# Hybrid decoder step on one core: a third key buffer, earlier gathers, closer decode steps and a re-spaced sample chain in the MLP

## Chip, cores and metric

One core of a Trainium2 chip runs the whole kernel. The metric is the device time of one execution in microseconds (us). Engines: PE is TensorE (PEld its weight loads), DVE is VectorE, ACT is ScalarE, POOL is GpSimd, SP is SyncE, which here only issues DMAs.

## What is computed

One layer of a decoder for two inputs at once: a prompt of 512 new tokens, and a sample of 8 sequences with one new token each, of which every one attends to 4096 cached tokens. Cut to what matters here:

```python
h = rmsnorm(x, g_pre_mix); q, k, v, logf, ..., gates = split(h @ w_in)
o_fox = forgetting_attention(q, k, v, logf)      # prompt: 512 x 512 causal
                                                 # sample: cache_k/cache_v[page_table], 4096 rows, 8 heads x 64
o_gla = gated_linear_attention(...)
u  = sigmoid(gfox) * (o_fox @ w_fox_out) + sigmoid(ggla) * (o_gla @ w_gla_out)
x  = x + rmsnorm(u @ w_o, g_post_mix)            # d_model 1024
h2 = rmsnorm(x, g_pre_mlp)
y  = x + rmsnorm(square(relu(h2 @ w_up)) @ w_down, g_post_mlp)   # d_ff 4096
```

Everything is float32. The paged cache that the sample reads is 8 x 32 pages of 128 rows, 64 MB of keys and 64 MB of values.

## The kernel before

**Dense work.** Every weight matrix is taken in units of 256 columns. A unit is loaded by SP (tile raw, four loads of 256 KB, up to two units ahead), split into a rounded high part (wh, ACT, L222) and the rest (wl, DVE, L223), and multiplied three times by PE (high x high, high x low, low x high) into PSUM tiles pmm. The MLP has four chunks c of 1024 hidden columns; each has an up half (four units, function up) and a down half (four units, function down). The prompt's 512 tokens are columns 0 to 511 of the transposed activations, and the 8 sample tokens can ride along as columns 512 to 519 where they are known in time.

**Decode.** The sample's attention to its cache is a Python generator, decode (from L549), of 144 steps: b counts 0 to 8, g 0 to 15. In a step with b < 8 the key page group of sequence b is gathered by POOL with an indirect DMA (tile kk, 512 KB, two buffers, L209), multiplied by the query (DVE, L574) and summed over the head dimension (DVE, L575). In a step with b > 0 the values of sequence b-1 are used: every second step one gathered value tile (tile kv, 1 MB, two buffers) goes through PE against the exponentials pt (tile pdv). So steps 1 to 128 have keys, and the last 16 have values alone. At the end of a sequence a chain over DVE, PE and ACT makes the exponentials (L604 to L621).

**How the steps are laid out among the dense work.** Each matmul adds its columns over 2400 to a planner's clock (L82). After each piece of dense work (a yield, in the MLP mostly 24 matmuls of 512 columns, so 5.12 us of that clock) pump(rate) pays clock x rate / TAU into an account and emits one decode step for each 1 in it; TAU is 3.1. The rates are PA to PD and PF before the MLP, PG = 1.5 in the first four yields of the MLP, and PE_ = 1 after them. LK and LV say how many steps ahead of its use a key or value gather is emitted (0 and 2). This is the order of emission. The framework then orders each engine's instructions by priority of emission, and lets a later one pass an earlier one whose inputs or buffer are not there yet in its own timeline; on the chip each engine runs that fixed order.

**The sample's path through the end.** When decode has ended, start_mix puts the generator sample_mix on the list side; beside(1) advances it once per yield of dense work. It projects the attention output with w_fox_out (four pieces) and w_o (four pieces), one per advance, with weights loaded again by SP into kv tiles (sload); then sample_post and sample_sum do the first norm and the residual sum, rsqrt (DVE and POOL, L217 and L218) the scale, and norm_T_sample (L333) scales x on DVE and transposes it in eight small PE transposes (L339) into h2S and, by split, into columns 512 to 519 of h2 and l2. From then on mixed[0] is true. Up units taken before that have no sample columns; they and the down units of the same chunk are put on the list late, and sample_mlp does them for the sample alone, one per advance, with the unit's weights loaded a second time into kv tiles (two loads of 512 KB each). The list whole marks a chunk of which any up unit was late; all four of its down units are then late too. sample_end, at the last down unit, drains the rest.

**Names of the rows.** px<-kv,c is a late unit's product on PE, px<-sel,td the sum over its four column groups, pd<-ident,qb the sample's transposes, pdv<-kv,pt decode's values, pmm<-h,wh and pmm<-wh,c and their like the dense units.

Of the kernel before, what the change touches and what calls it, by code (L numbers as in the profile page):

```python
# [17 lines left out]
D = 1024  # L18
T = 512
NB = 8  # L20
# [4 lines left out]
TS = T + NB  # L25
TR = 544
FP, LP, LQ = 3, 1, 1
PA, PB, PC, PD, PE_ = 1, 1.2, 0.6, 0.6, 1
LK, LV = 0, 2
TO = 1  # L30
PF, PG, HN = 0.8, 1.5, 2
BU = dict(h=4, c8=9, wh=6, wl=5, raw=5, kk=2, kv=2, td=2, ts=5, qb=2, tj=1, ev=1)
PK = 2
TAU = 3.1
MS = 1
# [15 lines left out]
def _emit(ctx, tc, I, O):  # L51
# [494 lines left out]
    oS = cst([128, 4, 32], "oS")  # L546
    G.memset(oS, 0.0)

    def decode():  # L549
        steps = [(b, g) for b in range(NB + 1) for g in range(NG)]  # L550
        pk, pv_ = [], []
# [1 line left out]
        lf = logf_load(0)  # L553
        bias = None
        for i, (b, g) in enumerate(steps):
            while nk <= min(i + LK, NB * NG - 1):
                pk.append(page_load(kvw, ixki, nk // NG, nk % NG, KJ, "kk"))
                nk += 1
            while nv <= NB * NV - 1 and NG + nv * VJ // KJ <= i + LV:
# [83 lines left out]
    def pump(rate):  # L643

        owed[0] += (clock[0] - seen[0]) * rate / TAU
        while owed[0] >= 1 and (scored[0] or count[0] < NG):
            owed[0] -= 1
            count[0] += 1
            if next(dec, "end") == "end":
                over[0] = True  # L650
        seen[0] = clock[0]
# [570 lines left out]
    def sample_mix():  # L1222
        x, y = new_["x"], new_["y"] = [[new([8, 512], "ts") for _ in range(2)] for _ in range(2)]
        V.tensor_scalar(out=sgf, in0=sgf, scalar1=0.5, scalar2=0.5, op0=ALU.mult, op1=ALU.add)
        acc = new([128, 2, 512], "kk")
        new_["acc"] = [acc[:, 0, :], acc[:, 1, :]]
        for i in range(2):
            nc.sync.dma_start(out=x[i], in_=I["x_sample"].rearrange("b l d -> (b l) d")[:, i * 512:(i + 1) * 512])
        for n in range(4):
            e, p = sproj(oS, sload(wfo, n * 256), "x")  # L1230
            for j in range(2):
                gsum_fm(e, j * 128, 128, p[:, j * 8:j * 8 + 8])
            sl = slice(2 * n, 2 * n + 2)
            V.tensor_tensor(out=uS[:, sl, 0:8], in0=p[:, 0:16].rearrange("p (a b) -> p a b", b=8), in1=sgf[:, sl, :],
                            op=ALU.mult)
            V.tensor_tensor(out=uS[:, sl, 0:8], in0=uS[:, sl, 0:8], in1=tgs[:, sl, :], op=ALU.add)
            yield
        for n in range(4):
            e, p = sproj(uS, sload(wo, n * 256), "x")
            gsum_tok(e, p[0:8, 0:256])  # L1240
            S.copy(out=half(y, n), in_=p[0:8, 0:256])
            yield
        sample_post(y, "g_post_mix", x)
        s2 = small([8, 1], "s2s")
        sample_sum(x, s2)
        yield
        rs = rsqrt(s2, 8, 1, 1.0 / D)
        norm_T_sample(x, rs, gpl, h2S)
        for i in range(2):
            split(h2S[:, 4 * i:4 * i + 4, 0:8], h2[i][:, :, T:TS], l2[i][:, :, T:TS])  # L1250
        mixed[0] = True
        side.append(("mlp", sample_mlp()))
        yield
# [18 lines left out]
            V.tensor_tensor(out=d, in0=p[:, 0:256], in1=d, op=ALU.add)  # L1272
        first[n] = False

    late, whole, mixed = [], [True] * 4, [False]

    def sample_mlp():

# [9 lines left out]
    def up(c, ah, al):  # L1288
# [7 lines left out]
        for n in range(4):  # L1296
            w = take()[0]
            with_sample = mixed[0] and not (c == 0 and n < HN)
            if not with_sample:
                whole[c] = False  # L1300
                late.append((wup, c, n))
            if c == 0 and n < HN:
                for r in (slice(0, 256), slice(256, 512)):
# [19 lines left out]
    def down(c):  # L1323
        def take_(n):
            w, _, raws = take()
            if not whole[c]:
                late.append((wdn, c, n))
            else:
                sample_acc(n, sproj_ps(aS[:, c * 8:c * 8 + 8, :], raws, "x"))
            if c == 3 and n == 3:  # L1330
                sample_end()
            return w
# [25 lines left out]
    def sample_end():  # L1358
        while not over[0]:
            owed[0] += 1  # L1360
            pump(0)
        start_mix()
        drain("mix", "mlp")
        y, x = new_["y"], new_["x"]
        for n in range(2):
            p = ps("x")
            mm(p[0:8, :], sel[:, 0:8], new_["acc"][n], True, True)
            S.copy(out=y[n][0:8, :], in_=p[0:8, :])
        sample_post(y, "g_post_mlp", x)
        for i in range(2):  # L1370
            nc.sync.dma_start(out=O["y_sample"].rearrange("b l d -> (b l) d")[:, i * 512:(i + 1) * 512], in_=x[i][0:8, :])

    def dense_mlp(gen, n, first=()):
        for i, _ in enumerate(gen):
            pump(first[i] if i < len(first) else n)
            if over[0]:
                start_mix()
            beside(MS)

    started = [False]  # L1380

    def start_mix():
        if not started[0]:
# [2 lines left out]

    yv = O["y_prompt"].rearrange("o (t p) d -> (o p) t d", p=128)
    acc2 = None
    for c in range(4):
        ah, al = [c8(F32R), c8(F32R)], [c8(F32R), c8(F32R)]  # L1390
        dense_mlp(up(c, ah, al), PE_, [PG] * (2 * HN if c == 0 else 0))
        if acc2 is None:
            acc2 = [c8(shape=[128, 2, 1024]), c8(shape=[128, 2, 1024])]
        if c == 3:
            ssp = small([128, 4, 4], "ssp", 2)
        dense_mlp(down(c), PE_)
# [27 lines left out]
```

## Time and profile before

| what | us |
|---|---|
| median of 3 runs | 1073.32 |
| lowest and highest of them | 1065.27, 1081.12 |
| the profiled execution | 1071.62 |
| its span, first to last instruction | 1069.9 |

The profiled execution is 1.7 us longer than its span and 1.7 us shorter than the median. Its mean granted clock of TensorE is 0.956 of full speed (2.4 GHz). A row of a timeline has start, duration, engine, line, operation, output<-inputs, shape and count, and in brackets the idle time of the engine before it with what ended that; a PE duration reaches from issue to the modelled end, and several overlap, so the pace is read from one start to the next. The 8 transposes, the sums and other float32 matmuls are shown as more than one record each.

### The profile page before, as it was taken

To read this page: it belongs to the slowest core of one execution; us is meant where nothing else is said; L and a number is where in the kernel's file an instruction comes from. 1 tells how busy PE (TensorE), PEld (TensorE's weight loads), DVE (VectorE), ACT (ScalarE), POOL (GpSimd) and SP (SyncE) were. 2 spreads that over 40 slices of the span, in tenths; PEclk is the share of its full clock that TensorE was granted. 3 is DMA by queue.
4 is the path that set the end of the run, shared out by engine and by line. 5 is a ranking of instruction groups with operands and counts; after the bars stand their busy time and mean duration, and the time that the engine had idled before them with its cause. 6 is when DMAs were issued, how large, how long until landed. Compare 5 with 4: busy or idle time off the path is not lost.

```text
span 1069.9 us, 20743 instructions
## 1 busy us (share of the span) xinstructions
PE 996.6 (93%) x8183; PEld 830.5 (78%) x8183; DVE 690.2 (65%) x1238; ACT 427.3 (40%) x1110; POOL 270.0 (25%) x256
## 2 busy tenths in 40 slices
PE   7998999999999899999894799999999799999996
PEld 5987867867977787797784678788787588888995
DVE  8577766867989858887669779567333333233356
ACT  6424544534833414333233444336313453115442
POOL 5232243353342313423334333430100000000001
PEclk9997999999999979999896899999999899999999
DMA  6746788587578638966994687994667366677222
GB/s 194 251 143 197 272 299 286 182 314 276 169 284 292 190 103 266 310 222 205 343 346 154 232 318 240 330 335 142 222 229 237 120 205 214 213 237 235 81 76 86
DMA packets 134279, 242.03 MB, mean 226 GB/s; under 512 B 11627, under 2 KB 105150, under 8 KB 125990
## 3 DMA queue, kind: packets, MB, share of 16 engines
q0 software_dynamic: 28032, 135.28, 36.0%
q1 hardware_dynamic: 106150, 105.43, 31.0%
q8 instruction: 64, 1.05, 0.4%
q14 instruction: 33, 0.27, 0.1%
HBM read 235.14 MB, written 5.47 MB: 225 GB/s over the span
## 4 chain that ended last, share of the span: by engine, by line
PE 56%; DMA 21%; DVE 12%; issue 7%; POOL 2%; ACT 1%; DVEq 0%; POOLq 0%; SPq 0%; ACTq 0%
PE pmm L85 41%; DMA kk<-in_cache_k,ixki 14%; PE px L85 8%; PE pdv L85 4%; DVE kk L574 3%; DMA kv<-in_cache_v,ixvi 3%; DVE sc L575 3%; DVE wl L223 2%; DMA raw<-in_w_in 1%; PE pd L85 1%; DMA kv<-in_w_up 1%; DMA kv<-in_w_down 1%; POOL kk L209 1%; DMA c<-in_state_gla 1%; POOL kv L209 1%
## 5 line engine op out<-in xcount | busy, mean ns | idle before, releaser
L85 PE MATMUL pmm<-h,wh 128*128 128x256 f32 (+2 forms) x1696 | 360.7, 308 | 8.6 <-ACT h L222 4.1
L85 PEld LDWEIGHTS pmm<-h,wh 128*128 128x128 f32 x1696 | 279.9, 196 | 45.5 <-issue 16.9
L85 PE MATMUL pmm<-h,wl 128*128 128x256 f32 (+2 forms) x848 | 258.8, 307 | 0.0
L209 POOL DMA_INDIRECT kk<-in_cache_k,ixki x128 | 162.6, 1270 | 334.8 <-DVE sc L575 205.7
L85 PE MATMUL pmm<-wh,c 128*128 128x256 f32 x1280 | 233.9, 283 | 5.5 <-DVE c L1040 3.6
L85 PEld LDWEIGHTS pmm<-wh,c 128*128 128x128 f32 x1280 | 197.2, 190 | 27.4 <-issue 16.9
L223 DVE TENSOR_TENSOR wl<-raw,wh 128x512 fp32r<-128x512 f32 x240 | 161.7, 686 | 80.8 <-PE pmm L85 56.0
L574 DVE TENSOR_TENSOR kk<-kk,qb 128x1024 f32<-128x1024 f32 x128 | 156.2, 1221 | 83.7 <-DMA kk<-in_cache_k,ixki 81.9
L222 ACT CAST wh<-raw 128x512 fp32r<-128x512 f32 x240 | 146.7, 619 | 157.2 <-PE pmm L85 96.2
L85 PE MATMUL pmm<-wl,c 128*128 128x256 f32 x640 | 179.2, 282 | 1.1 <-DVE wl L223 1.1
L85 PEld LDWEIGHTS pmm<-h,wl 128*128 128x128 f32 x848 | 165.1, 195 | 11.4 <-issue 4.6
L575 DVE TENSOR_REDUCE sc<-kk 128x16 f32<-128x1024 f32 x128 | 154.7, 1211 | 0.7
L85 PEld LDWEIGHTS pmm<-wl,c 128*128 128x128 f32 x640 | 120.8, 190 | 9.8 <-issue 7.9
L209 POOL DMA_INDIRECT kv<-in_cache_v,ixvi x64 | 70.4, 1100 | 146.7 <-PE pdv L85 124.4
L218 POOL TENSOR_TENSOR rs<-rs,mhalf 128x1 f32<-128x1 f32 (+2 forms) x21 | 16.3, 776 | 292.8 <-DVE rs L217 290.8
L85 PE MATMUL pdv<-kv,pt 128*32 128x512 f32 x512 | 68.0, 612 | 8.6 <-DMA kv<-in_cache_v,ixvi 8.5
L85 PE MATMUL pmm<-wh,h 128*128 128x256 f32 x384 | 74.8, 287 | 0.0
L85 PEld LDWEIGHTS pmm<-wh,h 128*128 128x128 f32 x384 | 59.8, 188 | 4.8 <-issue 4.6
L85 PE MATMUL pmm<-wl,h 128*128 128x256 f32 x192 | 55.7, 291 | 0.3 <-DVE wl L223 0.3
L1339 DVE TENSOR_TENSOR c<-pmm,c 128x256 f32<-128x256 f32 x48 | 18.7, 421 | 57.4 <-PE pmm L85 57.0
L1293 DVE TENSOR_TENSOR c<-td,c 128x256 fp32r<-128x256 f32 (+1 forms) x50 | 24.8, 497 | 32.6 <-ACT td L1292 32.4
L85 PE MATMUL pmm<-c,wh 128*128 128x512 f32 x128 | 42.7, 418 | 1.6 <-DVE c L911 0.9
(335 smaller groups left out, 1099.5 us busy)
## 6 DMA issues: line engine op xcount, KB each, us to landing
raw<-in_w_in SPq DMA_DIRECT2D x80, 256.0 KB
raw<-in_w_up SPq DMA_DIRECT2D x64, 256.0 KB
raw<-in_w_down SPq DMA_DIRECT2D x64, 256.0 KB
kv<-in_w_down SPq DMA_DIRECT2D x24, 512.0 KB
kv<-in_w_up SPq DMA_DIRECT2D x18, 512.0 KB
raw<-in_w_o SPq DMA_DIRECT2D x16, 256.0 KB
kv<-in_w_o SPq DMA_DIRECT2D x8, 512.0 KB
c<-in_x_prompt SPq DMA_DIRECT2D x4, 512.0 KB
```

The lines of the kernel that those rows point to most:

```text
L85: PE.matmul(out=out, lhsT=lhsT, rhs=rhs, start=start, stop=stop)
L209: G.indirect_dma_start(out=t, out_offset=None, in_=view, in_offset=bass.IndirectOffsetOnAxis(ap=ix[:, b, g:g + 1], axis=0))
L218: G.tensor_tensor(out=r, in0=a, in1=mhalf[:P, :n], op=ALU.pow)
L222: S.copy(out=hi, in_=raw)
L223: V.tensor_tensor(out=lo, in0=raw, in1=hi.bitcast(F32), op=ALU.subtract)
L574: V.tensor_tensor(out=K3, in0=K3, in1=qb[:, None, :].to_broadcast([128, KJ, 512]), op=ALU.mult)
L575: V.tensor_reduce(out=sc[:, g * 8 * KJ:(g + 1) * 8 * KJ], in_=K.rearrange("p (x d) -> p x d", d=64), axis=AX.X, op=ALU.add)
L1293: V.tensor_tensor(out=l, in0=r[:, 0:n], in1=d.bitcast(F32), op=ALU.subtract)
L1339: V.tensor_tensor(out=d, in0=p, in1=d, op=ALU.add)
```

## The change

The key tile kk gets a third buffer. PE_ goes from 1 to 1.25. From the beginning of the MLP a key gather is emitted one step ahead of its use (ahead[0] = LK + 1). Steps after the 128th, those with values alone, cost 0.5 of the account in place of 1. In sample_mix a bare yield is put ahead of sample_post, rsqrt is emitted right after sample_sum, and four yields stand between it and norm_T_sample, where one stood ahead of rsqrt; one more yield follows the transposes. A down unit is late only if an up unit of its own chunk is still on the list late (the list whole is gone), and catch_up puts sample_mlp back on the list side whenever something is late and nothing else is there.

```diff
--- before.py
+++ after.py
@@ -25,11 +25,11 @@
 TS = T + NB
 TR = 544
 FP, LP, LQ = 3, 1, 1
-PA, PB, PC, PD, PE_ = 1, 1.2, 0.6, 0.6, 1
+PA, PB, PC, PD, PE_ = 1, 1.2, 0.6, 0.6, 1.25
 LK, LV = 0, 2
 TO = 1
 PF, PG, HN = 0.8, 1.5, 2
-BU = dict(h=4, c8=9, wh=6, wl=5, raw=5, kk=2, kv=2, td=2, ts=5, qb=2, tj=1, ev=1)
+BU = dict(h=4, c8=9, wh=6, wl=5, raw=5, kk=3, kv=2, td=2, ts=5, qb=2, tj=1, ev=1)
 PK = 2
 TAU = 3.1
 MS = 1
@@ -546,6 +546,8 @@
     oS = cst([128, 4, 32], "oS")
     G.memset(oS, 0.0)
 
+    ahead = [LK]
+
     def decode():
         steps = [(b, g) for b in range(NB + 1) for g in range(NG)]
         pk, pv_ = [], []
@@ -553,7 +555,7 @@
         lf = logf_load(0)
         bias = None
         for i, (b, g) in enumerate(steps):
-            while nk <= min(i + LK, NB * NG - 1):
+            while nk <= min(i + ahead[0], NB * NG - 1):
                 pk.append(page_load(kvw, ixki, nk // NG, nk % NG, KJ, "kk"))
                 nk += 1
             while nv <= NB * NV - 1 and NG + nv * VJ // KJ <= i + LV:
@@ -643,8 +645,9 @@
     def pump(rate):
 
         owed[0] += (clock[0] - seen[0]) * rate / TAU
-        while owed[0] >= 1 and (scored[0] or count[0] < NG):
-            owed[0] -= 1
+        while owed[0] >= (1 if count[0] < NB * NG else 0.5) and (scored[0] or count[0] < NG):
+
+            owed[0] -= 1 if count[0] < NB * NG else 0.5
             count[0] += 1
             if next(dec, "end") == "end":
                 over[0] = True
@@ -1240,12 +1243,15 @@
             gsum_tok(e, p[0:8, 0:256])
             S.copy(out=half(y, n), in_=p[0:8, 0:256])
             yield
+        yield
         sample_post(y, "g_post_mix", x)
         s2 = small([8, 1], "s2s")
         sample_sum(x, s2)
+        rs = rsqrt(s2, 8, 1, 1.0 / D)
+        for _ in range(4):
+            yield
+        norm_T_sample(x, rs, gpl, h2S)
         yield
-        rs = rsqrt(s2, 8, 1, 1.0 / D)
-        norm_T_sample(x, rs, gpl, h2S)
         for i in range(2):
             split(h2S[:, 4 * i:4 * i + 4, 0:8], h2[i][:, :, T:TS], l2[i][:, :, T:TS])
         mixed[0] = True
@@ -1272,7 +1278,7 @@
             V.tensor_tensor(out=d, in0=p[:, 0:256], in1=d, op=ALU.add)
         first[n] = False
 
-    late, whole, mixed = [], [True] * 4, [False]
+    late, mixed = [], [False]
 
     def sample_mlp():
 
@@ -1297,7 +1303,6 @@
             w = take()[0]
             with_sample = mixed[0] and not (c == 0 and n < HN)
             if not with_sample:
-                whole[c] = False
                 late.append((wup, c, n))
             if c == 0 and n < HN:
                 for r in (slice(0, 256), slice(256, 512)):
@@ -1323,7 +1328,7 @@
     def down(c):
         def take_(n):
             w, _, raws = take()
-            if not whole[c]:
+            if not mixed[0] or any(v is wup and e == c for v, e, _ in late):
                 late.append((wdn, c, n))
             else:
                 sample_acc(n, sproj_ps(aS[:, c * 8:c * 8 + 8, :], raws, "x"))
@@ -1360,7 +1365,9 @@
             owed[0] += 1
             pump(0)
         start_mix()
-        drain("mix", "mlp")
+        drain("mix")
+        catch_up()
+        drain("mlp")
         y, x = new_["y"], new_["x"]
         for n in range(2):
             p = ps("x")
@@ -1375,9 +1382,14 @@
             pump(first[i] if i < len(first) else n)
             if over[0]:
                 start_mix()
+            catch_up()
             beside(MS)
 
     started = [False]
+
+    def catch_up():
+        if mixed[0] and late and not side:
+            side.append(("mlp", sample_mlp()))
 
     def start_mix():
         if not started[0]:
@@ -1386,6 +1398,7 @@
 
     yv = O["y_prompt"].rearrange("o (t p) d -> (o p) t d", p=128)
     acc2 = None
+    ahead[0] = LK + 1
     for c in range(4):
         ah, al = [c8(F32R), c8(F32R)], [c8(F32R), c8(F32R)]
         dense_mlp(up(c, ah, al), PE_, [PG] * (2 * HN if c == 0 else 0))
```

## Rows read from the trace of the kernel before

**Rows 1.** The page, busy time, share of the span and instructions of each engine.
```profile
PE 996.6 (93%) x8183; PEld 830.5 (78%) x8183; DVE 690.2 (65%) x1238; ACT 427.3 (40%) x1110; POOL 270.0 (25%) x256
```

**Rows 2.** Busy by stage: PE, PEld, DVE, ACT, POOL, clock, DMA share, GB/s.
```profile
600.00:735.00 135.00, 127.18 (x850) 104.06 (x851) 98.38 (x125) 53.63 (x121) 44.63 (x41) 0.97 0.83 292
735.00:795.00 60.00, 60.00 (x405) 47.75 (x404) 23.11 (x50) 23.15 (x51) 5.64 (x6) 1.00 0.62 211
848.00:991.00 143.00, 141.12 (x1257) 119.76 (x1250) 44.22 (x102) 51.24 (x131) 0.00 (x0) 0.98 0.68 214
```

**Rows 3.** The same columns, stretches of 10 us in the MLP.
```profile
600.00:610.00 10.00, 4.77 (x21) 3.11 (x22) 7.49 (x10) 3.31 (x8) 3.56 (x4) 0.74 0.82 278
...
690.00:700.00 10.00, 10.00 (x86) 8.07 (x85) 4.62 (x6) 2.50 (x5) 3.92 (x4) 1.00 1.01 374
...
840.00:850.00 10.00, 3.51 (x27) 2.08 (x27) 5.46 (x13) 5.25 (x14) 0.54 (x1) 0.68 0.03 8
850.00:860.00 10.00, 10.00 (x78) 9.28 (x77) 1.37 (x5) 3.64 (x12) 0.00 (x0) 0.81 0.51 164
```

**Rows 4.** Timeline of PE around the sample's transposes.
```profile
846.25 1.02 PE L339 MATMUL pd<-ident,qb 8*128 8x8 f32 x8 [6.17 <-DVE qb L336]
847.58 1.93 PE L85 MATMUL px<-kv,c 128*32 128x256 f32 x16 [0.32 <-DVE c L340]
...
850.47 0.63 PE L85 MATMUL pmm<-h,wh 128*128 128x256 f32 x2
...
851.11 0.63 PE L85 MATMUL pmm<-h,wh 128*128 128x256 f32 x2
...
853.93 0.51 PE L85 MATMUL px<-sel,td 128*128 128x8 f32 x4
...
856.05 1.07 PE L85 MATMUL px<-kv,c 128*32 128x256 f32 x16
...
857.50 0.40 PE L85 MATMUL pmm<-h,wh 128*128 128x256 f32 x2
...
857.85 0.40 PE L85 MATMUL pmm<-h,wh 128*128 128x256 f32 x2
```

**Rows 5.** DMA issues of the whole span: the late units' weights.
```profile
kv<-in_w_down SPq DMA_DIRECT2D x24, 512.0 KB
kv<-in_w_up SPq DMA_DIRECT2D x18, 512.0 KB
```

**Rows 6.** Key multiplications (L574) in a stretch: DVE, clock, DMA, GB/s.
```profile
590.00:733.00 143.00, 34.34 (x28) 0.97 0.81 285
```

**Rows 7.** Waits from 600 to 735 us: total, times, longest.
```profile
POOL kk L209 <- DVE sc L575: 49.9, 19, 6.7
DVE kk L574 <- DMA kk<-in_cache_k,ixki: 24.5, 15, 4.8
...
ACT wh L222 <- DMA raw<-in_w_up: 10.9, 2, 6.4
```

**Rows 8.** Waits from 0 to 600 us.
```profile
DVE kk L574 <- DMA kk<-in_cache_k,ixki: 57.4, 42, 4.1
```

**Rows 9.** Waits of PE over the whole span.
```profile
PE px L324 <- DVE c L1185: 7.1, 1, 7.1
...
PE pmm L85 <- DVE c L1040: 3.6, 2, 3.4
```

**Rows 10.** The chain that ended last: start, us, what.
```profile
490.64 8.74 DMA kk<-in_cache_k,ixki
```

**Rows 11.** Timeline of PE at the MLP's start.
```profile
605.23 1.94 PE L85 MATMUL pdv<-kv,pt 128*32 128x512 f32 x8 [5.69 <-DMA kv<-in_cache_v,ixvi]
```

**Rows 12.** Timeline of POOL in the steps with values alone.
```profile
755.36 0.94 POOL L209 DMA_INDIRECT kv<-in_cache_v,ixvi  x1 [28.07 <-PE pdv L85]
...
764.09 0.94 POOL L209 DMA_INDIRECT kv<-in_cache_v,ixvi  x1 [6.55 <-PE pdv L85]
...
773.08 0.94 POOL L209 DMA_INDIRECT kv<-in_cache_v,ixvi  x1 [5.14 <-PE pdv L85]
```

## Prediction

> **What bounds the kernel now.** I read the page first: PE is busy 93% of the span, DVE 65%, the rest far less [rows 1]. So the end moves only where PE stands still, or works on something that the change takes away; an earlier decode is worth nothing by itself. The second view is the busy time by stage. In the last key steps (600 to 735 us) PE is busy 127 of 135 us, DVE 98, and the DMA engines 83%; in the steps with values alone (735 to 795) PE never stops; in the stretch that catches up on late units (848 to 991) it stands for 2 of 143 us [rows 2]. Third, 10 us at a time, the MLP shows two holes: 600 to 610, where PE is busy 4.8 us at clock 0.74, and 840 to 850, busy 3.5 us at 0.68, with a clock of 0.81 in the ten after that [rows 3]. Everything else in the MLP is a PE that has work. The reader is to see there that the holes are short and that the part around them is full.
>
> The hole at 840 is the sample's transposes: PE stands 6.17 us for the scaled x from DVE [rows 4], because the last weight sum, the norm, the residual, the second norm and the scaling follow each other over ACT, DVE and POOL, and the next dense matmuls need the very columns that these transposes make. The hole at 600 is a value tile: 5.69 us for a gather [rows 11].
>
> **The change part by part.**
>
> *Transposes.* Emitted five yields later, they have some 10 to 28 us of dense work ahead of them (yields of 2.56 or 5.12 us) against a stall of 6.17 us. What goes is more than the stall, since PE comes out of it at half speed: the late product takes 1.93 us against 1.07 us later, and three dense matmuls of 256 columns 0.64 us (850.47 to 851.11) against 0.35 us (857.50 to 857.85) [rows 4]. From about 849.4 to 853.9 us that is 4.5 x (1 - 0.35/0.64) = 2.0 us. Sum: 6.2 + 0.3 (the idle behind the transposes) + 0.9 + 2.0 = 9.4 us. Cover: the transposes now belong to the down half of chunk 1, whose dense work needs no sample columns. If the cover is gone, because decode ends so late that the chain is still running when chunk 2's first up unit wants its sample columns, all 9.4 us stay.
>
> *Fewer late units.* By the planner's clock, a yield of 5.12 us pays 5.12 x 1.5 / 3.1 = 2.48 steps in the first four yields and 1.65 after them. I start from 100 steps done at the MLP's start: 28 key multiplications stand in the trace from 590 us on [rows 6]. Before, 45 calls are left (the last ends the generator): 9.9 in four yields, 35 more at 1.65 (0.83 in the four short yields of a down half), so decode ends in emission in chunk 1's down half, second yield; ten advances of the mix later, in chunk 2's first up yield, mixed is true. That leaves 9 up units and 12 down units late, and the issues agree: 18 and 24 loads, two for each [rows 5]. After: 9.9, then 2.06 per yield until step 128 (nine yields), then 4.13; the end falls in the first yield of chunk 1's up half, and 15 advances later, in the seventh yield of its down half, mixed is true, with 8 up and 8 down units late. Five late units fewer. The up unit costs at most 1.07 + 2 x 0.51 = 2.1 us on PE [rows 4] and rides along at almost nothing; I take 1 us. The four down units cost PE the same either way; what goes is four times two loads and a share of 2 us of idle in 143 us [rows 2]; I take 0.5. Sum 1.5 us, bounds 0 and 4.
>
> *Third key buffer.* It works in the whole kernel, since POOL's gather waits not for its place in the order but for the buffer that the sum two steps back frees: 49.9 us of waiting in 19 waits in 600 to 735 [rows 7]. One more buffer issues every gather about a step earlier. DVE waits 57.4 us for keys in 42 waits before 600 us [rows 8] and 24.5 in 15 waits after that [rows 7], and what stands behind such a multiplication on DVE (splits, residues of the mix) is late with it. But PE feels little of that: its waits on DVE that name work behind a key gather are 3.6 us for c L1040, right behind the gather of 8.74 us [rows 9, 10], and perhaps the 7.1 us for c L1185 [rows 9], where DVE itself is full. Upper bound for the gain 3.6 + 7.1 and half as much again for the slow clock behind them, 16 us; lower bound 0; nearest row the 3.6 us: I take 4 us. A new order of DVE's instructions can also go wrong by as much as one such wait, 7 us; that stays in the range.
>
> The Trainium skill, page "DMA: Bandwidth & Descriptors", section "Anatomy of one DMA — SWDGE (gpsimd) path", puts a gather from GpSimd at 2.0 us and its bytes over 436 GB/s, by which 512 KB would take an estimated 3.2 us. By that two buffers would do, the third be worth 0 in place of 4 us, and the sum 4 us higher. The trace has 8.74 us for such a gather [rows 10], so I go by the row.
>
> *Closer steps, gathers ahead.* In 600 to 733 us 28 key steps take 143 us, 5.1 us each [rows 6], where emission asks for 3.1 us of clock or less: decode is behind its emission already, held by gathers. A rate of 1.25 hence asks for what isn't there; only the third buffer can deliver. Its limit is DMA: 135 us at 292 GB/s [rows 2] are 39.4 MB, and at the 374 GB/s of a full ten [rows 3] they take 105 us. So key steps end at best 25 to 30 us sooner, near 710 us. DVE has 98 us of work there [rows 2]; 28 steps with two instructions of 1.2 us (34.34 us for one of them [rows 6]) are 69 of it, the other 29 shrink with the stretch to 23, so 92 us in 105: nearly full, where it was 73%. The cost is what the weights wait longer: ACT's 10.9 us in two waits [rows 7] is the nearest row, of which PE felt none in the full tens. Bounds 0 and 11 us; I take 2.
>
> *Values twice as dense.* They come no faster: POOL issues them in pairs 9 us apart (755.36, 764.09, 773.08), each time after PE has freed a buffer [rows 12]. With two value tiles that is 4.5 us per tile, where emission asked for 6.2 us of clock already and will ask for 2.5. Worth 0 in time, but it moves the end in emission forward, which the count above has in it. What is late next: real decode then ends at about 770 us, where emission has it at some 725; the mix runs without yields to pace it, twelve loads of 512 KB over two buffers. At about 3.5 us each that is 42 us, and the chain of 9 us behind it ends near 820, some 7 us before chunk 2's up half wants the columns. That is close, and is the third rival.
>
> *The hole at 600.* Nothing in the change gives a value buffer or an earlier value gather; 0, with bounds of -8 (5.69 us and its slow clock) and 0.
>
> **The sum.** Against the profiled execution: -9.4 - 1.5 - 4 + 2 = -12.9 us, so 1071.6 - 12.9 = 1058.7 us. The median of the runs shown is 1.7 us above that execution, so I forecast 1060 us, 1.2% less.
>
> **The rivals.**
> 1. The buffer works in the whole kernel: DVE's waits of 57 and 24 us go, both named PE waits with their slow clock (16 us) and the hole at 600 (8 us) too. -9.4 - 1.5 - 16 - 8 = -35 in full, or 1038 from the median; with half of the last two -23, or 1050. For it: gathers are the longest single pieces of the chain. Against: PE hid nearly all of those waits. I put it at 1045.
> 2. The stall doesn't go but moves: sample columns are late at chunk 2's first up unit, as real decode lags its emission by 45 us. Then -1.5 for the late units, and the buffer's 4 us and its price nearly even out: about 1071. For it: the margin of 7 us. Against: ten yields sufficed before.
> 3. The weights starve, the other side. Three key and two value gathers in flight stand against 256 KB weight loads while the DMA engines are full (1.01 of their time in 690 to 700 us [rows 3]). A wait of ACT of 6.4 us [rows 7] then comes with every unit; with the unit or so that is split ahead PE feels perhaps half, 3 us in each of ten units between 600 and 712 us, and the clock falls behind the holes. 30 + 10 - 11 gives +29, or 1100 us; it decides from ACT's waits for weights over some 35 us in that stretch. Against it: in the full tens PE had none.
>
> **How the numbers follow.** The forecast has a chance of 0.48, rival 1 0.22, rival 2 0.21, rival 3 0.09. The range: 1040 us takes most of rival 1; 1082 holds rival 2 with the spread of the runs (8 us either way), and leaves most of rival 3 outside. Two per cent, about what a measurement of this kernel can tell from no change, is 21.5 us, so faster means under 1052: nine tenths of rival 1 and a fifth of the forecast, 0.29. Slower means over 1095: somewhat over half of rival 3, 0.05. The rest, 0.66, is within.
>
> **What would show it.** Right: no PE idle before L339; 16 loads of kv from w_up and 16 from w_down; the last key multiplication near 710 us, the last value product near 765; DVE's waits for keys less than half of 82 us; PE still over 93% busy. Wrong: PE idle of 5 us or more ahead of the transposes or of the first matmul of 264 columns; ACT's waits for weights over 35 us in the key steps; PE waits for value gathers of several us each in the dense value steps; a key zone as long as before.

## The result

| | us (median, lowest to highest) | ratio to the kernel before, 95% interval |
|---|---|---|
| before, in the runs beside the change | 1073.86 (1065.27 to 1081.12) | |
| the change | 1094.88 (1091.04 to 1097.51) | 1.0241 [1.0202, 1.0280] |

2.4% slower; forecast were 1060 us with a range of 1040 to 1082. (The two medians alone give 1.0196, just under that interval; by either the time lies above the range.) The profiled execution of the change took 1096.37 us, its span 1094.7, at a mean clock of 0.940. Its page answers to [rows 1] with

```profile
PE 1006.8 (92%) x8211; PEld 831.4 (76%) x8211; DVE 690.1 (63%) x1241; ACT 427.8 (39%) x1116; POOL 280.7 (26%) x256
```

Of the 24.8 us by which the span grew, 10.2 are PE's busy time, for nearly the same matmuls at a lower clock, and 14.6 its idle time (87.9 against 73.3 us). To see where, I take three rows from the views of single lines and tiles; each ends with the first and the last start of its group. Before:

```profile
L574 DVE TENSOR_TENSOR kk<-kk,qb x128: 1189/1224/1295, 37.8 to 730.9; 128x1024 f32<-128x1024 f32 x128
L1290 ACT ACTIVATE td<-pmm x50: 366/385/601, 605.9 to 1008.7; 128x256 f32<-128x256 f32 x36, 128x512 f32<-128x512 f32 x14
L638 DVE TENSOR_TENSOR oS<-ntmp,lv x2: 215/217/219, 794.3 to 794.5; 64x32 f32<-64x32 f32 x2
```

After:

```profile
L576 DVE TENSOR_TENSOR kk<-kk,qb x128: 1201/1219/1277, 40.3 to 629.2; 128x1024 f32<-128x1024 f32 x128
L1296 ACT ACTIVATE td<-pmm x52: 362/384/607, 649.9 to 1033.5; 128x256 f32<-128x256 f32 x40, 128x512 f32<-128x512 f32 x12
L640 DVE TENSOR_TENSOR oS<-ntmp,lv x2: 206/208/211, 782.4 to 782.6; 64x32 f32<-64x32 f32 x2
```

The reader is to see three dates in them. The last key multiplication is 102 us sooner. The first evacuation of the MLP, and so the MLP's start, is 44.0 us later. Decode's end, the write of oS, is only 12 us sooner. From the MLP's start to the end of the span it took 464.0 us before and takes 444.8 now: 44.0 lost ahead of the MLP, 19.2 won in it, where no key step is left to do.

The keys run ahead of the dense work from the beginning. Windows of the key multiplications alone (columns: DVE busy with their count, clock, DMA share, GB/s), before and after:

```profile
100.00:200.00 100.00, 23.37 (x20) 1.00 0.77 264
200.00:300.00 100.00, 23.17 (x19) 0.98 0.69 239
600.00:700.00 100.00, 24.08 (x20) 0.97 0.86 301
```

```profile
100.00:200.00 100.00, 29.68 (x25) 0.90 0.76 255
200.00:300.00 100.00, 28.02 (x24) 1.00 0.82 291
600.00:700.00 100.00, 8.54 (x7) 0.88 0.58 197
```

What that does to the dense work is plainest at 80 to 120 us. All engines by window, with the columns of [rows 2], before and after:

```profile
80.00:100.00 20.00, 17.06 (x112) 13.93 (x112) 15.57 (x23) 7.81 (x20) 5.08 (x5) 0.68 0.67 208
100.00:120.00 20.00, 20.00 (x172) 17.82 (x172) 15.16 (x29) 9.93 (x32) 7.23 (x6) 1.00 0.69 218
```

```profile
80.00:100.00 20.00, 6.44 (x30) 4.85 (x29) 15.51 (x29) 1.90 (x3) 8.60 (x7) 0.67 0.65 215
100.00:120.00 20.00, 12.31 (x70) 9.02 (x70) 17.68 (x24) 4.61 (x12) 7.60 (x6) 0.56 0.61 189
```

PE stands for 18 us more of these 40, while DVE is hardly busier than it was. DVE's timeline shows with what. Before, the end of the forget gate's chain (L378, L379, tiny instructions for the sample's and the prompt's log decay) has one multiplication and two sums of keys between its pieces:

```profile
69.59 0.25 DVE L378 SCALAR_TENSOR_TENSOR lf<-lf,lf 8x8 f32<-8x8 f32 x2
69.77 1.20 DVE L575 TENSOR_REDUCE sc<-kk 128x16 f32<-128x1024 f32 x1
...
73.92 1.23 DVE L574 TENSOR_TENSOR kk<-kk,qb 128x1024 f32<-128x1024 f32 x1 [2.87 <-DMA kk<-in_cache_k,ixki]
...
76.47 0.15 DVE L379 SCALAR_TENSOR_TENSOR lfs<-lf,lf 8x8 f32<-8x8 f32 x1
```

After, every piece or two stands behind a key multiplication or a key sum, and such a multiplication waits for its gather with the chain queued behind it:

```profile
74.48 0.25 DVE L378 SCALAR_TENSOR_TENSOR lf<-lf,lf 8x8 f32<-8x8 f32 x2
76.65 1.22 DVE L576 TENSOR_TENSOR kk<-kk,qb 128x1024 f32<-128x1024 f32 x1 [1.92 <-DMA kk<-in_cache_k,ixki]
77.80 1.21 DVE L577 TENSOR_REDUCE sc<-kk 128x16 f32<-128x1024 f32 x1
78.92 0.25 DVE L378 SCALAR_TENSOR_TENSOR lf<-lf,lf 8x8 f32<-8x8 f32 x2
...
86.64 1.22 DVE L576 TENSOR_TENSOR kk<-kk,qb 128x1024 f32<-128x1024 f32 x1 [1.59 <-DMA kk<-in_cache_k,ixki]
...
91.95 0.15 DVE L379 SCALAR_TENSOR_TENSOR lfs<-lf,lf 8x8 f32<-8x8 f32 x1
...
98.72 1.22 DVE L576 TENSOR_TENSOR kk<-kk,qb 128x1024 f32<-128x1024 f32 x1 [1.94 <-DMA kk<-in_cache_k,ixki]
...
101.51 0.18 DVE L379 SCALAR_TENSOR_TENSOR lft<-lf,lf 128x32 f32<-128x32 f32 x1
```

lfs is written at 91.95 us, not at 76.47. The weight splits wl are in the same queue, and so PE waits for them; its waits from 60 to 130 us (total, times, longest), before and after:

```profile
PE pmm L85 <- DVE wl L223: 0.3, 1, 0.3
```

```profile
PE pmm L85 <- DVE wl L223: 9.6, 4, 3.2
```

The loads of the weights hang on the same splits, which free the tile raw: from 60 to 130 us SP waits 33.1 us in four waits for wl (before 2.7 us in one, and 19.5 us in another for lf, L378), and ACT waits 28.1 us for weights where it waited 20.1. Over the whole span PE's largest named wait is now for value gathers: 19.8 us in 8 waits, all ahead of the MLP, where it was 8.5 us in 4.

Two of the predicted steps did come. The late units are 16 up and down loads each [rows 5], and the transposes [rows 4] have no idle time ahead of them:

```profile
kv<-in_w_up SPq DMA_DIRECT2D x16, 512.0 KB
kv<-in_w_down SPq DMA_DIRECT2D x16, 512.0 KB
```

```profile
855.12 0.66 PE L339 MATMUL pd<-ident,qb 8*128 8x8 f32 x8
```

### The profile page after: what moved, and what is told of

It reads as the page before. It is cut to its first block, busy times and chain, and to the rows that moved or that the text cites. A ratio compares the mean times of both kernels' runs of the same rounds, so it can differ in the third digit from the quotient of the medians.

```text
span 1094.7 us, 20812 instructions
## 1 busy us (share of the span) xinstructions
PE 1006.8 (92%) x8211; PEld 831.4 (76%) x8211; DVE 690.1 (63%) x1241; ACT 427.8 (39%) x1116; POOL 280.7 (26%) x256
## 4 chain that ended last, share of the span: by engine, by line
PE 62%; DMA 14%; issue 10%; DVE 8%; POOL 4%; ACT 1%; POOLq 0%; DVEq 0%; SPq 0%; ACTq 0%
PE pmm L85 47%; DMA kk<-in_cache_k,ixki 9%; PE px L85 7%; PE pdv L85 5%; DMA kv<-in_cache_v,ixvi 4%; POOL kk L209 2%; DVE kk L576 2%; DVE sc L577 2%; PE pd L85 1%; POOL rs L218 1%; DVE wl L223 1%; PE px L688 1%; POOL kv L209 1%; DMA kv<-in_w_fox_out 0%; DVE c L1355 0%
## 5 line engine op out<-in xcount | busy, mean ns | idle before, releaser
L85 PE MATMUL pmm<-h,wh 128*128 128x256 f32 (+2 forms) x1728 | 362.1, 306 | 12.1 <-ACT wh L222 3.6
L85 PEld LDWEIGHTS pmm<-h,wh 128*128 128x128 f32 x1728 | 283.2, 195 | 42.9 <-issue 13.3
L85 PE MATMUL pmm<-h,wl 128*128 128x256 f32 (+2 forms) x864 | 261.9, 306 | 7.6 <-DVE wl L223 7.6
L85 PE MATMUL pmm<-wh,c 128*128 128x256 f32 x1280 | 228.4, 280 | 0.0
L85 PEld LDWEIGHTS pmm<-wh,c 128*128 128x128 f32 x1280 | 195.5, 188 | 13.9 <-issue 10.9
L85 PEld LDWEIGHTS pmm<-h,wl 128*128 128x128 f32 x864 | 167.5, 195 | 24.8 <-issue 10.9
L85 PE MATMUL pmm<-wl,c 128*128 128x256 f32 x640 | 178.1, 279 | 1.0 <-DVE wl L223 1.0
L85 PEld LDWEIGHTS pmm<-wl,c 128*128 128x128 f32 x640 | 120.2, 188 | 6.3 <-issue 4.2
L209 POOL DMA_INDIRECT kv<-in_cache_v,ixvi x64 | 75.7, 1183 | 187.7 <-PE pdv L85 164.4
L85 PE MATMUL pdv<-kv,pt 128*32 128x512 f32 x512 | 82.3, 661 | 19.9 <-DMA kv<-in_cache_v,ixvi 19.8
L85 PE MATMUL pmm<-wh,h 128*128 128x256 f32 x384 | 76.9, 291 | 0.0
L85 PEld LDWEIGHTS pmm<-wh,h 128*128 128x128 f32 x384 | 61.4, 192 | 5.2 <-issue 4.9
L85 PE MATMUL pmm<-wl,h 128*128 128x256 f32 x192 | 55.5, 291 | 2.8 <-DVE wl L223 2.8
L85 PEld LDWEIGHTS pdv<-kv,pt 128*32 128x32 f32 x512 | 12.8, 112 | 41.6 <-DMA kv<-in_cache_v,ixvi 25.8
```

The lines of the kernel that those rows point to most:

```text
L85: PE.matmul(out=out, lhsT=lhsT, rhs=rhs, start=start, stop=stop)
L209: G.indirect_dma_start(out=t, out_offset=None, in_=view, in_offset=bass.IndirectOffsetOnAxis(ap=ix[:, b, g:g + 1], axis=0))
```

## The experiments

All are timed against the kernel before on the same chip; there it took 1070 to 1074 us. "MLP" in the table is the first start of td<-pmm and the stretch from there to the end of the span, "oS" the end of decode; both read from each run's rows as above.

| run | key buffers | median us | ratio, interval | MLP from, for | oS |
|---|---|---|---|---|---|
| the change | 3 | 1094.9 | 1.0241 [1.0202, 1.0280] | 649.9, 444.8 | 782.6 |
| e1 the change, two key buffers | 2 | 1095.3 | 1.0218 [1.0179, 1.0258] | 609.4, 486.8 | 782.0 |
| e2 before, three key buffers | 3 | 1098.3 | 1.0261 [1.0223, 1.0298] | 644.8, 451.7 | 811.0 |
| e3 the change, third buffer for the MLP's gathers alone | 2, then 3 | 1091.2 | 1.0175 [1.0132, 1.0218] | 612.1, 477.6 | 778.0 |
| e4 the sample's chain and the late rule alone | 2 | 1060.7 | 0.9925 [0.9897, 0.9952] | 603.0, 454.5 | 790.2 |
| e5 e1 and own tile for the mix's copies | 2 | 1073.7 | 1.0013 [0.9988, 1.0037] | 606.1, 468.4 | 796.8 |
| e6 the change and own tile | 3 | 1083.1 | 1.0107 [1.0048, 1.0167] | 641.2, 438.3 | 784.9 |
| e7 e1, last values at full price | 2 | 1086.7 | 1.0120 [1.0049, 1.0191] | 606.0, 479.4 | 791.2 |
| e8 e4 and own tile | 2 | 1061.2 | 0.9915 [0.9891, 0.9939] | 605.7, 455.3 | 793.1 |
| e10 before, third buffer from the 49th gather on | 2, then 3 | 1122.9 | 1.0463 [1.0400, 1.0526] | 666.5, 456.4 | 835.2 |
| e13 e1, mix nine yields later | 2 | 1062.3 | 0.9904 [0.9851, 0.9956] | 603.3, 456.7 | 794.6 |
| e14 e2, gathers paced by the dense work | 3 | 1081.7 | 1.0104 [1.0052, 1.0155] | 607.4, 474.4 | 808.9 |
| e15 before, gathers paced in the same way | 2 | 1129.6 | 1.0508 [1.0481, 1.0536] | 650.9, 481.6 | 860.9 |
| e16 e4 with three buffers, paced | 3 | 1069.7 | 1.0020 [0.9990, 1.0050] | 600.2, 465.5 | 803.8 |
| e17 the change, mix nine yields later | 3 | 1093.7 | 1.0182 [1.0150, 1.0214] | 644.3, 447.4 | 788.0 |

### The parts of the change, one at a time

```diff
e1 (the change, but)
+BU = dict(... kk=2, ...)
e2 (before, but)
+BU = dict(... kk=3, ...)
e3 (e1, with one buffer kb more)
+pk.append(page_load(..., "kb" if ahead[0] > LK and nk % 3 == 0 else "kk"))
e4 (the change, but kk=2, PE_=1, no gathers ahead, every step at the price of 1)
```

> The changed kernel with two key buffers again, all its other edits kept. Theory A (the third buffer lets decode run ahead of the dense work in the whole kernel, which costs some 45 us before the MLP, while the other edits save 10 to 20 in it): the MLP starts at about 600 us again and the time is 1050 to 1066 us, 1 to 2% under the kernel before. Rival B (the higher rate and the dense values in the MLP are what costs): 1090 us or more. Rival C (both parts cost): 1074 to 1090 us.

> The kernel before with a third key buffer and nothing else. Theory A: key multiplications run ahead, 118 or more of 128 before 600 us in place of 102; the MLP starts 35 to 50 us later, and the time is 1095 to 1120 us, since the MLP's gains are missing. Rival B: within 5 us of the kernel before, 1069 to 1079 us.

> The changed kernel, but with the third key buffer used from the beginning of the MLP alone (two before it). Theory A: before the MLP as the kernel before, key steps end near 710 us, and the time is 1045 to 1065 us. If a third buffer costs in the MLP as well, it is slower than the changed kernel with two buffers by 5 us or more.

> The kernel before with the sample's chain re-spaced and the new rule for late units alone: two key buffers, rate 1, no gathers ahead, values at full price. By the count of the prediction 11 up and 12 down units are late (22 and 24 loads). If the stall ahead of the transposes goes as reckoned (9.4 us) and nothing else changes, 1062 to 1067 us; if the stall only moves, 1071 to 1078 us.

e2 came as expected, and e4 but for 1.3 us under its range: the third buffer alone costs 2.6%, the sample's chain and the late rule alone win 0.75%, 8 us. e1 and e3 were misses: without the third buffer, or with it for the MLP's gathers alone, the time should have come back, and e1 is no better than the change, with an MLP that starts nearly as early as before and lasts 487 us. (e1 lies in the band of its rival B, the steps themselves; e13 below speaks against that reading. And e3 doesn't quite keep the third buffer to the MLP: its tile kb is free from the start, so the first gather into it goes out at 10.5 us and the first multiplication from it comes at 482.8.) So there are two losses, and the second was hidden behind the first. e2's rows show the first one, without anything else of the change:

```profile
L574 DVE TENSOR_TENSOR kk<-kk,qb x128: 1199/1219/1283, 40.1 to 623.3; 128x1024 f32<-128x1024 f32 x128
L1290 ACT ACTIVATE td<-pmm x50: 356/384/601, 644.8 to 1035.2; 128x256 f32<-128x256 f32 x36, 128x512 f32<-128x512 f32 x14
```

The second is in e1 at 721 to 786 us. ACT's timeline there: the evacuation of an up unit (L1296), then none for 62 us, and the next right behind the first copy of the sample's mix (L309).

```profile
721.93 0.60 ACT L1296 ACTIVATE td<-pmm 128x512 f32<-128x512 f32 x1 [5.54 <-PE pmm L85]
...
777.15 0.59 ACT L596 COPY ev<-pdv 128x512 f32<-128x512 f32 x1 [28.92 <-PE pdv L85]
783.45 0.37 ACT L309 COPY td<-px 128x256 f32<-128x256 f32 x1 [5.71 <-PE px L85]
783.72 0.60 ACT L1296 ACTIVATE td<-pmm 128x512 f32<-128x512 f32 x1
```

PE meanwhile issues its last dense product at 738.07 us, since nobody empties the PSUM tiles that it has filled, and does the end of decode by itself, one value tile after another:

```profile
738.07 0.40 PE L85 MATMUL pmm<-h,wl 128*128 128x512 f32 x1
743.22 0.38 PE L612 MATMUL pdv<-ident,mx 128*8 128x128 f32 x1 [4.75 <-DVE mx L609]
...
755.95 1.94 PE L85 MATMUL pdv<-kv,pt 128*32 128x512 f32 x8 [4.18 <-DMA kv<-in_cache_v,ixvi]
...
775.15 1.94 PE L85 MATMUL pdv<-kv,pt 128*32 128x512 f32 x8 [1.94 <-DMA kv<-in_cache_v,ixvi]
...
782.30 1.94 PE L85 MATMUL px<-kv,oS 128*32 128x256 f32 x16 [1.37 <-DVE oS L640]
```

```profile
740.00:760.00 20.00, 6.91 (x31) 1.57 (x35) 4.48 (x13) 2.92 (x17) 2.80 (x3) 0.63 0.40 136
760.00:780.00 20.00, 11.18 (x48) 2.59 (x40) 0.20 (x2) 0.59 (x1) 2.80 (x3) 0.50 0.74 257
```

Both the mix's copies and the up units' evacuations go to the tile td, which has two buffers. With the higher rate and the half price, decode ends in emission in the first yield of chunk 1's up half by the prediction's count, and the mix's copies are emitted from there on. They can run only when decode has really ended. Whatever is emitted behind them and wants td waits for them.

### Two ways to take the second loss away

```diff
e5 (e1) and e6 (the change; there tm has one buffer)
-e = new([128, 256], "td")
+e = new([128, 256], td)     # "tm" where sample_mix and sample_post call, also for gslice
e13 (e1) and e17 (the change), at the head of sample_mix
+for _ in range(9):
+    yield
e7 (e1): each step costs 1 of the account
```

> The kernel after with two key buffers, as in the run before, and the sample's projection copies (L309 in sample_mix) and norm slices in a tile of their own, tm, in place of the tile td that the prompt's up units use for their evacuation (L1296). Theory M (decode's end is emitted ahead of where it really is, and the mix's copies, two td buffers, then stand in front of the up units' copies until decode has ended, so that PE runs out of dense work for some 45 us): ACT's L1296 goes on between 722 and 784 us, PE has dense work beside the last values, and the median falls from 1095 to 1045-1062 us. Rival (the closer steps themselves cost: gathers and weights starve PE whatever the order of the copies): 1085 us or more. Between 1062 and 1085: both have a share.

> The kernel after as it is (three key buffers) with the mix's copies and norm slices in a tile of their own (tm, one buffer, for room). Theory (two separate losses, of which this takes away the second; the first is the third key buffer's, whose keys run ahead of the dense work before the MLP): the MLP still starts near 645 us, the stretch from there to the end gets shorter than the 440 us of after, 415 to 432 us, and the median is 1068-1087 us. Rival 1 (after's only loss is the third buffer; the tile td costs nothing there): 1090-1098. Rival 2 (the tile is all of it): 1045-1062.

> The kernel after with two key buffers and steps of values alone at the full price of 1 (so decode's end is emitted in the fifth yield of chunk 1's up half, where it was in the first). Theory M (the loss is the distance between the emitted and the real end of decode): the dense work runs four yields or some 20 us further before it is blocked, the stall of some 45 us shrinks to 15-28, and the median is 1066-1082 us. Rival (rate 1.25 itself, by gathers against weights): 1088 or more. If the price of 0.5 was the whole loss: under 1062.

> The kernel after with two key buffers (1095 us in its run above) and nine bare yields at the head of sample_mix, so that its projections are emitted behind decode's real end and the sample's columns exist from the sixth yield of chunk 2's up half (11 up and 12 down units late, as in the run with the sample's chain and the late rule alone, 1061 us). The rate of 1.25, the gathers ahead and the half price of the last values all stay. Theory M (the whole loss of the closer steps is that the mix stands in the program's order ahead of where decode really ends; nothing is wrong with the steps themselves): no stall between 728 and 860 us, median 1057-1068 us. Rival (closer steps and denser values cost by themselves): 1075 or more.

e5 won 21.6 us and lies between its two bounds, where both theory and rival have a share. The stall at 738 to 785 us is gone, and another has come: with dense work no longer blocked, the mix now comes too late for chunk 2's up half. In PE's timeline it waits for the mix's weights one after another, then for the scaled x, with no dense work left that wants no sample columns:

```profile
827.08 0.64 PE L85 MATMUL px<-kv,c 128*32 128x256 f32 x8 [2.36 <-DMA kv<-in_w_o]
...
832.27 1.08 PE L85 MATMUL px<-kv,c 128*32 128x256 f32 x8 [1.80 <-DMA kv<-in_w_o]
...
842.57 1.02 PE L339 MATMUL pd<-ident,qb 8*128 8x8 f32 x8 [7.70 <-DVE qb L336]
```

```profile
820.00:840.00 20.00, 8.98 (x69) 3.72 (x67) 3.69 (x8) 4.62 (x12) 0.56 (x1) 0.73 0.62 193
840.00:860.00 20.00, 15.82 (x125) 12.27 (x126) 2.52 (x12) 4.38 (x18) 0.54 (x1) 0.76 0.42 134
```

e13 moves the mix, not the tile: nine yields later in emission, with the rate of 1.25, the gathers ahead and the half price all kept. PE then never stops in the steps with values alone, as before [rows 2]:

```profile
735.00:795.00 60.00, 60.00 (x421) 48.68 (x420) 23.03 (x50) 19.68 (x46) 5.61 (x6) 1.00 0.58 202
```

It took 1062.3 us, as much as e4 without any of these, and with the same late units (22 and 24 loads). That settles the second loss: with two buffers the closer steps, the gathers ahead and the dense values together cost nothing by themselves, and win nothing; what cost was that the mix stood in the program's order ahead of where decode really ends. oS is written between 778 and 797 us in all of e1, e3, e4, e5, e7, e8 and e13, whatever the rate. e7 missed its range by 5 us: the end is emitted four yields later and the time falls by 9 us only, with five late units more than e1 (18 and 24 loads, where e1 has 16 and 16). e8 shows the reverse: where the mix is emitted late enough, the tile of its own is worth nothing.

> The sample's chain and the late rule of the change alone (1061 us above), with the mix's copies and norm slices in a tile of their own. Theory M: with two buffers and rate 1 the emitted end stands some 10 yields later than in the change, behind the real end, so nothing is blocked and the tile is worth nothing: 1056-1066 us. If the shared tile costs here too: 1045-1056.

### How much of the second loss is in the change itself

> The whole change with three key buffers and nine bare yields at the head of sample_mix, which took the loss of the closer steps away with two buffers (1062 us). What is left is the third buffer's loss alone beside the gain of the sample's chain. Theory (two separate losses): MLP starts near 645 us as in the change, median 1078-1092 us, 16 to 30 above the run with two buffers. Rival 1 (with the mix in its place the keys done early are paid back in the MLP): 1060-1072. Rival 2 (the third buffer is the whole loss of the change, the order of the mix nothing): 1093 or more.

A miss: 1093.7 us, just in the band of the second rival. With three buffers the last keys are long done, the value gathers are ahead, and the same block on ACT lasts only from the last dense product to the mix's first copy:

```profile
778.79 0.58 ACT L596 COPY ev<-pdv 128x512 f32<-128x512 f32 x1 [1.50 <-PE pdv L85]
783.87 0.37 ACT L309 COPY td<-px 128x256 f32<-128x256 f32 x1 [4.49 <-PE px L85]
784.14 0.60 ACT L1296 ACTIVATE td<-pmm 128x512 f32<-128x512 f32 x1
```

PE is without dense work from 776.8 to 786.0 us there, 9 us. e17 wins these back and, as it seems, gives them away again: its columns come later, so it has 22 and 24 late loads, seven late units more. e6, which lifts the block and keeps the 16 late units, is 11.8 us under the change and 10.6 under e17. So a late unit costs an estimated 1.1 to 1.5 us (10.6 / 7 by the medians; the ratios differ by 0.0075, which is 8 us or 1.1 each). That is argued and not shown: the two runs differ also in where the mix stands, and their intervals overlap a little. e6 itself came as expected. And the two parts multiply out: e2 x e4 = 1.0261 x 0.9925 = 1.0184, against 1.0182 for e17 and 1.0241 for the change, whose intervals overlap. The change's loss is the third key buffer's, less the gain of the sample's chain; the block of 9 us and the late units saved seem to go nearly even.

### Is it the run-ahead that the third buffer costs?

The order of DVE's program is fixed before the kernel runs, so it can be counted. The table has the key multiplications that stand ahead of the weight split wl that n of the 240 splits precede.

| n | before | e2 | the change | e14 | e10 |
|---|---|---|---|---|---|
| 24 | 15 | 27 | 27 | 15 | 18 |
| 56 | 53 | 71 | 71 | 57 | 58 |
| 88 | 79 | 110 | 110 | 84 | 98 |
| 128 | 110 | 128 | 128 | 108 | 128 |
| 152 | 126 | 128 | 128 | 127 | 128 |

In the change they stand as in e2, so the run-ahead is the buffer's work, not the rate's. e14 puts the order nearly back with three buffers, e15 is the control with two (shortened; the fourth gather is the first to have the copy):

```diff
e14 (e2) and e15 (before), in page_load, ahead of a key gather
+G.tensor_copy(out=t[:, 0:1], in_=newest_wl[:, 0, 0:1].bitcast(F32))
```

> The kernel before with a third key buffer, and ahead of each key gather (from the fourth on) POOL copies one element per partition of the newest weight split (wl) into the key tile. So a gather can't start before the dense work has come to the place at which the gather is emitted; the buffer count stays three. In DVE's program order 84 key steps then stand ahead of weight split 88 and 108 ahead of split 128, where it is 79 and 110 with two buffers and 110 and 128 with three and no such copy. Theory (the third buffer costs by letting the keys run ahead of the dense work): the MLP starts at 590-610 us as before, in place of 637, and the median is 1060-1082 us in place of 1098. Rival (three gathers in flight cost by themselves, by DMA or by DVE's share): 1090 or more.

> Control for the paced third buffer (1082 us): the same copy from the newest weight split ahead of each key gather, with two key buffers as before. Theory (the copy itself, which holds POOL's queue for dense work, costs what is left of the loss): 1077-1088 us, the third buffer without run-ahead is worth about 0. Rival (three gathers in flight cost 10 us by themselves): 1066-1075.

```profile
L576 DVE TENSOR_TENSOR kk<-kk,qb x128: 1187/1220/1269, 40.5 to 730.5; 128x1024 f32<-128x1024 f32 x128
L1292 ACT ACTIVATE td<-pmm x50: 367/385/604, 607.4 to 1020.5; 128x256 f32<-128x256 f32 x36, 128x512 f32<-128x512 f32 x14
L210 POOL COPY kk<-wl x125: 173/268/3350, 49.3 to 722.3; 128x1 f32<-128x1 f32 x125
```

In e14 the MLP starts at 607 us, nearly as before, and 17 of e2's 28 us are back (1098.3 - 1081.7). PE's waits for value gathers, 8.5 us in 4 before and 22.5 us in 11 in e2, are 6.5 us in 5. Three gathers in flight with the keys in nearly their old places cost 11 us, the copy's price included, so the larger part of the loss is the run-ahead. The copy holds back the gathers and with them the multiplications, so e14 doesn't part what the place on DVE costs from what the earlier transfers cost. The control was a miss: the copy alone, with two buffers, costs 5%, since POOL waits in its queue for the dense work, then for a buffer, and DVE waits 146.6 us for keys. So the copy is no free instrument, and what it costs in e14 stays open; with it, the third buffer is worth 48 us. What is left in e14 may be the copy's price or the third gather's own, and no run shows which.

> The sample's chain and the late rule of the change alone (1061 us above), with a third key buffer held to the pace of the dense work by the copy from the newest weight split. Theory (run-ahead is the third buffer's only harm, and PE hides nearly all waits for keys): 1054-1068 us, the buffer worth -5 to +5. If the waits for gathers did cost PE time, as the prediction's first rival had it: 1035-1052. If three gathers in flight cost by themselves: 1075 or more.

e16 lands 2 us over its range, 9 over e4: the paced third buffer has no gain to add to the sample's chain either.

```diff
e10 (before, with kk=2 and one buffer kb more)
+pk.append(page_load(..., "kb" if nk >= 48 and nk % 3 == 0 else "kk"))
```

> The kernel before, with a third key buffer that is used only from the 49th gather on, by every third gather. Theory (the loss of 25 us with three buffers arises in two places: some 20 us between 72 and 118 us, where key multiplications stand in front of the forget gate's chain on DVE, and some 40 between 284 and 530 us, of which about half comes back in the MLP): the first place is as before, 8% of the dense columns are done by 90-98 us, the second loses still, and the median is 1072-1088 us. Rival 1 (any run-ahead of the keys costs the same, wherever it arises): 1094 us or more. Rival 2 (only the first place matters, the rest is given back in the MLP): 1062-1072.

A miss: 1122.9 us is 35 us over its range and in the band of rival 1. Only the first half of the theory held. I count PE's records of products into pmm and add up their columns: 8% of them are done at 92 us before, 113 in e2 and 96 in e10, so the first place of the loss is nearly gone where the third buffer is not yet in use. But the whole is dearer than with three buffers throughout. From 24 to 36% of the columns (the linear attention, with many short instructions on DVE) it takes 152 us with 23 key steps in it before, 172 with 34 in e2, and 202 with 37 in e10. By the table e10 has fewer keys ahead of split 88 than e2 (98 against 110) and is 25 us slower, so the count alone doesn't give the loss; why three more keys cost 30 us in that stretch, no run tells. PE's largest named wait over that run is for value gathers, 26.4 us in 8 waits. As in e3, the first gather into kb goes out at 10.5 us, long before its turn.

No version was found that beats e4 (1060.7, 1.0% to 0.5% under before); e8 and e13 are equal to it.

## Why the prediction was wrong

- **Third key buffer: wrong, and the step that failed.** It was "I take 4 us" of gain, bounds 0 and 16, with 7 for a new order gone wrong. Alone it costs 2.6%, 28 us. The step asked which waits for gathers would go, and they went: DVE waits 48.7 us for keys before 600 us where it was 57.4 [rows 8]. PE's waits grew elsewhere instead: for wl from 0.3 to 9.6 us (60 to 130 us), for value gathers from 8.5 to 19.8 us. The step did not ask where the keys that come sooner would be placed. I took the place of a key step for a matter of emission; it is a matter of when its data can be there, and with a third buffer 110 of them stand ahead of split 88, not 79. Each takes 2.4 us of DVE, in which the dense work's own chains have to wait. That PE hid nearly all of the waits was right, and was the reason not to touch them.
- **Closer steps: the size was near (2 us; in e13, with the gathers ahead and the dense values, about nothing), the worth of it not.** That the rate delivers nothing without the third buffer held: with two buffers the last key multiplication comes at 737 in e1, 733 in e5 and 731 in e13, where it was 731 before, and the 1.25 changes the emitted end alone. With the third buffer for the MLP's gathers (e3) it comes at 711, near the 710 that the working named, and the time is 1091 us all the same. In the change the keys end at 629, since most of them are done ahead of the MLP.
- **Values twice as dense: costed at 0, and the second step that failed.** "They come no faster" held, and decode's end stayed near 790 us. But the count that let it end in emission in chunk 1's up half gave the mix a place ahead of dense work which then had to wait for it. I looked for this only as late columns at chunk 2's up half (rival 2 of the list, which the working of this step calls the third). That came true in e5, where the mix's chain ended at 842 us, not near 820. In e1 the block came sooner, by way of the tile td, which the working does not mention; e1 takes 33 us longer than e13, which has the mix behind it. In the change PE stands without dense work for 9 us.
- **Transposes, -9.4 us: near.** No idle ahead of them, and e4, with this and the late rule alone, is 8 us under before.
- **Fewer late units: the count of 8 and 8 was right, the price probably not.** 1.5 us for five was 0.3 each; e6 against e17 gives an estimated 1.1 to 1.5 each, which no run isolates. e4 has 23 late units in place of 21, and so two more to pay for.
- **The hole at 600: 0, as taken.** PE's wait for a value gather, 5.69 us [rows 11], is there still, 6.49 us at 624 us.
- **Rival 3, the slow side,** had weights starve in the MLP by DMA. In the change ACT's waits for weights from the MLP's start on (645 to 785 us) are 15.0 us in five waits, under the 35 that it named: not that. Before 600 us they grew from 20.5 to 31.0 us; from 60 to 130 us the loads themselves wait for wl, as above, while the DMA engines are no busier from 80 to 120 us than before (0.65 and 0.61 of their time, 0.67 and 0.69 before).
- **The signs.** Two came: no idle ahead of L339, 16 and 16 loads. Three of the others failed: the last key at 629 us (near 710 was named), DVE's waits for keys at 48.7 us before 600 us alone (under half of 82), and PE's share at 92% (over 93).

## What to carry to other kernels

One more buffer for a transfer that is off the critical path can do more than take its wait away: in this kernel, whose engines' orders are planned by when data can be there, it moved the work on that data forward, in front of work that the bounding engine waits for. So count, before and after, what stands ahead of what in the program of the engine that both share. And when a generator of side work is sped up, compare its emitted end with its real end: everything emitted in between that waits for the real end, and shares a tile or a queue with the main work, can become a stop for the main work, as the mix did in e1.

## What was not expected of the hardware

With PE doing nothing but decode's last values (e1, 756 to 775 us), six 1 MB gathers follow each other every 3.84 us ((775.15 - 755.95) / 5), 273 GB/s, while in the full ten of [rows 3] the DMA engines moved 374. The pace is that of the two buffers: from issue to landing the gathers issued at 761.87 and 769.65 us took 5.50 and 5.46 us, the products on the tile 1.9 us more, and so one buffer's round is 7.78 us (769.65 - 761.87), or 3.9 us for each of two. PE, idle for half of that time, was given the lower clock (0.50, so 1.2 GHz, in the window of 760 to 780 us): eight products of 512 columns took 1.94 us, against 1.06 us in the change, where dense work ran beside them (row L85 pdv<-kv,pt x8 at 770.54 us).

By the rule of the Trainium skill, page "DMA: Bandwidth & Descriptors", section "Anatomy of one DMA — SWDGE (gpsimd) path", one gather of 1 MB would take an estimated 4.4 us (2.0 and the bytes over 436 GB/s). Here it took 5.5 us, with the other buffer's gather in flight for part of that time; no run shows one alone.
